# Reordering the first expert selection, its gathers and the first U weights around the query projection

## The chip, the cores and the metric

The kernel runs on one core of one Trainium2 chip. The metric is the device time of one execution in microseconds (us). The engines are PE (matmul; PEld is its weight load), DVE, ACT, POOL and SP, which issues most of the DMAs.

## The reference, cut to what matters

One decoder layer: a token mixer, then a layer of single-neuron experts, then a final norm. Only the expert layer is touched.

```python
qh = (xb @ w_query).reshape(128, 8, 2, 128)          # 8 heads, two halves of a query
s = einsum('thpd,hpnd->thpn', qh, sub_keys)          # scores against 2 x 128 keys of a head
sv, si = top_k(s, 16)                                # the best 16 keys of each half
cand = sv[..., 0, :, None] + sv[..., 1, None, :]     # 16 x 16 sums
cidx = si[..., 0, :, None] * 128 + si[..., 1, None, :]
top_s, pos = top_k(cand, 16); eidx = take(cidx, pos) # 16 experts of each head
gate = softmax(top_s)
act = gelu(einsum('thkd,td->thk', expert_u[eidx], xb))
y = einsum('thk,thkd->td', gate * act, expert_v[eidx])
```

## The kernel before

576 tokens reach the expert layer. For 192 of them (block 0 with 128 tokens, block 1 with 64) the rows of U and V are gathered by index with indirect DMAs that POOL issues. For the other 384 all 16384 experts are computed densely: 128 half steps, each with one chunk of 128 experts of U (function `hidden`), then 128 half steps over V (`experts`), with the gates scattered into a dense array. Every float32 product is made of three matmuls on a high and a low part: ACT copies the weight to the high part, and DVE or POOL subtracts it from the raw weight to get the low part.

`scored` comes just ahead of `hidden`. It goes over two segments of tokens, first 320 (which hold blocks 0, 1 and 2), then 256 (blocks 3 and 4, `o == 0`). In each it goes over 16 chunks `c` of `w_q`: SP loads the raw weight (tag `wr`, 3 buffers), ACT makes `wh` (L133), POOL makes `wl` (L134; DVE does it for the first four chunks of the first segment), PE makes the query (L1092, L1093, then L1095 which needs `wl`), ACT copies it to `qT` (L1097), PE makes the scores of the chunk before (`psc`, L1068), ACT copies them to `sc` (L1071), and DVE finds the best 16 (`top16`, L1020 to L1028, two passes of eight). The instructions here are ordered by the compiler's scheduler, by the order in which they stand in the program and by when it reckons them ready; `after` adds an order by hand.

`select(0)` stands between the two segments: DVE builds candidate sums (L1128 to L1132), takes the best 16 of them (`tv`, `ti`), turns positions into ranks (L1147 to L1158), and looks up the key indices by comparing ranks with 0..15 (`eq`, L1168), multiplying with the indices that ACT has spread out (`sbx`, L1167, in the buffer of `cand`; L1171) and adding in halves (L1177). The softmax (Exp on ACT at L1142, then L1181 to L1183 and L1190) and the indices `gi` (L1189) end it, and four `gather_begin` follow. After the 16th chunk of the second segment, `fetch`, `hi` and `lo` load the first three chunks of U and split them (`lo` of the third is left to `hidden`, where half step h makes the low part of half step h + 2, L1440).

`in_order` fixes the order of PE, DVE, ACT and SP from `hidden` on to that of the program. In each half step `fill` lets DVE do pieces of gathered rows (L1346, L1353) and of the selection of the other blocks, by a written-out cost, ahead of `lo`. At the end, three blocks of 128 output rows are normed: Square on ACT (L1598), a scale, the product on DVE in two halves (L1603), and the output DMAs (L1605), one by SP and one by ACT.

Of the kernel before, what the change touches and what calls it, by code (L numbers as in the profile page):

```python
# [9 lines left out]
F32 = mybir.dt.float32  # L10
F32R = mybir.dt.float32r
BF = mybir.dt.bfloat16
# [10 lines left out]
P = 128  # L23
# [98 lines left out]
class Net:  # L122
# [907 lines left out]
    def scored(self):  # L1030
# [23 lines left out]
        with self.pool("keys", 1, side="right") as kp, self.pool("qw", 2, side="right") as wp:  # L1054
            keys = kp.tile([P, 2 * PH, NK], F32, name="keys")
            nc.sync.dma_start(keys, I["keys"])
            for o, w in SEG:
                here = [b for b, (t0, n) in enumerate(self.blks) if o <= t0 < o + w and b != 1]

                first = 2 * P if o + w == NT else w  # L1060

                def scores(c, q):
                    h, x = divmod(c, 2)
                    pc = self.ps.tile([P, 3, NK], F32, name="psc", tag="ps")
                    sc = wp.tile([P, 2, NK], F32, name="sc", tag="sc", bufs=12)
                    for y, b in enumerate(here):
                        t = (self.blks[b][0] - o) if b else first
                        self.after(mm(pc[:, y, :], q[:, t:t + P], keys[:, c, :], start=True, stop=True), self.last_mm)  # L1068
                    if o + w == NT:
                        self.after(mm(pc[:, 2, :], q[:, P:2 * P], keys[:, c, :], start=True, stop=True), self.last_mm)  # L1070
                    nc.scalar.activation(sc, pc[:, :2], AF.Copy)  # L1071
                    for y, b in enumerate(here):
                        self.top16(P, wp, (sc[:, y, :], sv[:, b, h, x, :], si[:, b, h, x, :]))
                    if o + w == NT:
                        g, k = divmod(h, HB)
                        if g == 0:
                            held[k, x] = wp.tile([P, NK], F32, name="sch", tag="sch", bufs=2 * HB)
                        t, sl = held[k, x], slice(g * NX, (g + 1) * NX)
                        nc.scalar.activation(t[sl], pc[sl, 2], AF.Copy)
                        if g == XG - 1:  # L1080
                            self.top16(P, wp, (t, sv[:, 1, k, x, :], si[:, 1, k, x, :]))

                held = {}
                prev = None
                for c in range(2 * PH):
                    wh, wl = self.weights(I["w_q"][c], lo=nc.vector if o and c < 4 else nc.gpsimd)
                    q = wp.tile([P, 3 * P], F32, name="qT", tag="qT")
                    pq = self.pz.tile([P, 512], F32, name="pq", tag="acc")
                    xs = [(self.xg[0][k], self.xg[1][k]) if o + w == NT else (self.x2h[k][:, o:o + w], self.x2l[k][:, o:o + w])
                          for k in range(KC)]  # L1090
                    for k, (xh, xl) in enumerate(xs):
                        mm(pq[:, :w], wh[:, k, :], xh, start=k == 0, stop=False)  # L1092
                        mm(pq[:, :w], wh[:, k, :], xl, start=False, stop=False)  # L1093
                    for k, (xh, xl) in enumerate(xs):
                        self.last_mm = mm(pq[:, :w], wl[:, k, :], xh, start=False, stop=k == KC - 1)  # L1095
                    n = P + NX if o + w == NT else w
                    nc.scalar.activation(q[:, :n], pq[:, :n], AF.Copy)  # L1097
                    if o + w == NT:
                        nc.scalar.activation(q[:, n:], pq[:, P:w], AF.Copy)
                    if prev:  # L1100
                        scores(*prev)
                    prev = (c, q)
                if o == 0:
                    for s in range(3):
                        self.fetch(s)
                        self.hi(s)
                        if s < 2:
                            self.lo(s)
                scores(*prev)
                if o + w == NT:  # L1110
                    for _ in self.select(0):
                        pass
                    for _ in range(4):
                        self.gather_begin()
                    for d, v in ((self.x2h, self.xg[0]), (self.x2l, self.xg[1])):
                        for k in range(KC):
                            nc.sync.dma_start(d[k][:, o:].bitcast(F32), v[k][:, :MD - o].bitcast(F32))

    def select(self, b):

        nc, wp, sv, si = self.nc, self.sp, self.sv, self.si
        n, H = P, HB if b == 1 else PH
        f = H / PH
        s0, s1 = sv[:n, b, :H, 0, :], sv[:n, b, :H, 1, :]
        cd = wp.tile([P, H, NCAND], F32, name="cand", tag="cand")
        nc.vector.tensor_tensor(cd[:n, :, :TOPK], s0[:, :, 0:1].to_broadcast([n, H, TOPK]), s1, op=ALU.add)  # L1128
# [10 lines left out]

        g = wp.tile([P, H, TOPK], F32, name="gate", tag="gate", bufs=2)  # L1140
        nc.vector.tensor_tensor(g[:n], tv[:n], tv[:n, :, 0:1].to_broadcast([n, H, TOPK]), op=ALU.subtract)
        nc.scalar.activation(g[:n], g[:n], AF.Exp)  # L1142

        def small(name, dt=BF):
            return wp.tile([P, H, TOPK], dt, name=name, tag=name)
# [12 lines left out]
        nc.vector.tensor_add(a[:n], a[:n], t[:n])  # L1158
        yield 1.3 + f
        out = []  # L1160
        sbs = wp.tile([P, H, 2, TOPK], BF, name="sb", tag="sb")
        nc.vector.tensor_copy(sbs[:n], si[:n, b, :H])
        for x, rank in enumerate((a, r)):
            sb = sbs[:, :, x, :]
            e = wp.tile([P, H, TOPK, TOPK], BF, name="eq", tag="eq")
            sx = wp.tile([P, H, TOPK, TOPK], BF, name="sbx", tag="cand")
            nc.scalar.activation(sx[:n], sb[:n, :, :, None].to_broadcast([n, H, TOPK, TOPK]), AF.Copy)  # L1167
            nc.vector.tensor_tensor(e[:n], rank[:n, :, None, :].to_broadcast([n, H, TOPK, TOPK]),  # L1168
                                    self.io16[:n, None].to_broadcast([n, H, TOPK, TOPK]), op=ALU.is_equal)
            yield 0.2 + 1.1 * f  # L1170
            nc.vector.tensor_tensor(e[:n], e[:n], sx[:n], op=ALU.mult)  # L1171
            yield 0.1 + 1.05 * f
            w = TOPK
            v = small(f"ix{x}")
            while w > 1:
                w //= 2
                nc.vector.tensor_add(e[:n, :, :w, :] if w > 1 else v[:n, :, None, :], e[:n, :, :w, :], e[:n, :, w:2 * w, :])  # L1177
                yield (w * H * TOPK) * 0.53e-3 + 0.15
            out.append(v.rearrange("p h k -> p (h k)"))
        sm = wp.tile([P, H], F32, name="gsum", tag="gsum")  # L1180
        nc.vector.tensor_reduce(sm[:n], g[:n], axis=AX.X, op=ALU.add)  # L1181
        nc.vector.reciprocal(sm[:n], sm[:n])
# [1 line left out]
                                       op0=ALU.mult, op1=ALU.mult)  # L1184
        g = g.rearrange("p h k -> p (h k)")
        if b < 2:
            gi = self.gi[b]
            for x in range(2):
                nc.vector.scalar_tensor_tensor(gi[:, x, :], out[x], float(NK), out[1 - x], op0=ALU.mult, op1=ALU.add)  # L1189
            nc.vector.tensor_copy(gi[:, 2, :].bitcast(F32), g)  # L1190
        self.sel[b] = (*out, g)
        yield 1.0

# [118 lines left out]
    def gather_begin(self):  # L1312


        nc = self.nc
        s = self.gstep
        if s == NROW:
            return
        assert s < 4 * GL or 1 in self.sel
        self.gstep += 1  # L1320
        runs = [(0, k) for k in range(4)] + [(1, k) for k in range(XK // GL)] + [(0, k) for k in range(4, PH * TOPK // GL)]
        if s < GL:
            kind, k, r = "u", 0, s
        elif s < 2 * len(runs) * GL - GL:
            k, r = divmod((s - GL) // 2, GL)
            kind, k = ("v", k) if s % 2 else ("u", k + 1)
        else:
            kind, k, r = "v", len(runs) - 1, s % GL
        z, k = runs[k]
        c = k * GL + r  # L1330
        t = self.gp.tile([P, D], F32, name="gr", tag="gr")
        x = 0 if kind == "u" else 1
        src = self.I["v"].rearrange("j i k d -> (j i) (k d)") if x else self.I["ur"]
        nc.gpsimd.indirect_dma_start(out=t, out_offset=None, in_=src,  # L1334
                                     in_offset=bass.IndirectOffsetOnAxis(ap=self.gi[z][:, x, c:c + 1], axis=0))
        self.rows.append((t, kind, z, k, r, c))

    def gather(self):

# [95 lines left out]
            self.ws[s] = [w, None]  # L1435

    def lo(self, s):
        if s < 2 * NK:
            w = self.ws[s][1] = self.up.tile([P, KC, P], F32R, name="ul", tag="ul", bufs=3)
            self.nc.vector.tensor_sub(w, self.raws.pop(s), self.ws[s][0].bitcast(F32))  # L1440

# [88 lines left out]
    def experts(self):  # L1530
# [5 lines left out]
        with ExitStack() as es:  # L1536
# [53 lines left out]
            for b in range(nb):  # L1590
# [10 lines left out]
                for c in range(2):  # L1601
                    sl = slice(c * 512, (c + 1) * 512)
                    nc.vector.scalar_tensor_tensor(o[:, sl], py[b][:, c, :], v, self.gf[:, sl], op0=ALU.mult, op1=ALU.mult)  # L1603
                    if b:
                        (nc.scalar if c else nc.sync).dma_start(self.O["yg"][b * P - ND:(b + 1) * P - ND, sl], o[:, sl])  # L1605
                    else:

                        for n0, n1 in ((16, P), (ND, 16)):
# [98 lines left out]
```

## Time and profile before

| | |
|---|---|
| median of 3 runs | 1939.73 us (1939.11 to 1944.89) |
| the profiled execution | 1941.62 us, its span 1939.4 us |
| PE busy | 1889.3 us (97%) |
| DVE busy | 1592.7 us (82%) |
| ACT busy | 909.2 us (47%) |
| POOL busy | 745.1 us (38%) |
| the chain that ended last | PE 78%, DMA 11%, DVE 9% |

All moments below are us from the start of the span. The second segment of `scored` runs from about 722 to 794 and `hidden` from there to about 1377. A busy share is an average over stages; an engine can be idle for most of the span and still be the one that the others wait for in one stage.

### The profile page before, as it was taken

The page shows a single profiled execution, that of the slowest core. Times are in us where ns is not written, and L with a number is a line of the kernel's source. Part 1 is how long each engine was busy: PE and PEld are TensorE (multiplying, and loading weights), DVE is VectorE, ACT ScalarE, POOL GpSimd, SP SyncE. Part 2 cuts the span into 40 slices and gives each one's busy share as a digit, 9 for nine tenths or more (in the row PEclk, how much of TensorE's full clock was granted, in tenths as well). Part 3 has the DMA queues.
Part 4 walks back from the last instruction along what each step waited for, and adds up shares of the span by engine and source line. Part 5 has one row for each costly group of instructions (what it writes and reads, how often), then busy time and mean ns, then how long its engine had stood idle before and what let it go on. Part 6 is the DMA issues. An engine that isn't in the chain of part 4 may idle for free.

```text
span 1939.4 us, 31893 instructions
## 1 busy us (share of the span) xinstructions
PE 1889.3 (97%) x11759; PEld 1722.4 (89%) x11759; DVE 1592.7 (82%) x2962; ACT 909.2 (47%) x1598; POOL 745.1 (38%) x535
## 2 busy tenths in 40 slices
PE   8999999999999997999999999999999999999997
PEld 7998999788999897999999999999888888877786
DVE  6686776676365779999999999798999888988887
ACT  5542334262324554544878899633333333333333
POOL 1110010300001256345444444366676565665650
PEclk9999999999999998999999999999999999999999
DMA  7355343465554644799999999999999999999992
GB/s 267 103 158 156 87 112 100 140 190 181 175 166 149 211 130 158 248 343 332 348 354 344 398 396 380 376 401 397 402 400 401 397 399 402 400 398 401 399 401 103
DMA packets 219780, 548.08 MB, mean 283 GB/s; under 512 B 31474, under 2 KB 95730, under 8 KB 217960
## 3 DMA queue, kind: packets, MB, share of 16 engines
q1 hardware_dynamic: 163896, 344.17, 50.2%
q0 software_dynamic: 55296, 201.35, 27.0%
q8 instruction: 92, 1.51, 0.3%
q10 hardware_dynamic: 432, 0.54, 0.1%
q14 instruction: 64, 0.52, 0.1%
HBM read 474.89 MB, written 69.77 MB: 281 GB/s over the span
## 4 chain that ended last, share of the span: by engine, by line
PE 78%; DMA 11%; DVE 9%; issue 1%; ACT 1%; SPq 0%; DVEq 0%; ACTq 0%
PE py L1546 18%; PE pz L138 9%; PE pz L140 9%; PE pz L139 9%; PE acc L138 4%; PE acc L140 4%; PE acc L139 4%; DMA wr<-in_v 4%; DMA wj<-wd 3%; PE pw L1264 2%; PE py L664 1%; PE pz L659 1%; PE pq L1095 1%; PE pq L1092 1%; PE pbr L138 1%
## 5 line engine op out<-in xcount | busy, mean ns | idle before, releaser
L1334 POOL DMA_INDIRECT gr<-in_ur,gi x192 | 302.8, 1577 | 265.1 <-DVE yt L1353 200.7
L1334 POOL DMA_INDIRECT gr<-in_v,gi x192 | 300.6, 1566 | 238.8 <-DVE gr L1346 177.3
L1434 ACT ACTIVATE uh<-wr 128x1024 fp32r<-128x1024 f32 x256 | 270.2, 1056 | 217.8 <-PE py L1546 109.7
L138 PE MATMUL pz<-x2h,uh 128*128 128x384 f32 x1024 | 347.0, 339 | 0.0
L140 PE MATMUL pz<-x2h,ul 128*128 128x384 f32 x1024 | 342.9, 335 | 0.0
L139 PE MATMUL pz<-x2l,uh 128*128 128x384 f32 x1024 | 342.9, 335 | 0.0
L1440 DVE TENSOR_TENSOR ul<-wr,uh 128x1024 fp32r<-128x1024 f32 x256 | 313.5, 1225 | 8.9 <-PE pz L140 3.9
L1353 DVE SCALAR_TENSOR_TENSOR yt<-gr,ga,yt 128x1024 f32<-128x1024 f32 x192 | 246.1, 1282 | 7.1 <-DMA gr<-in_v,gi 6.0
L1346 DVE SCALAR_TENSOR_TENSOR gr<-gr,xt 128x1024 f32<-128x1024 f32 x192 | 234.7, 1224 | 12.2 <-DMA gr<-in_ur,gi 12.0
L138 PE MATMUL acc<-xnh,wh 128*128 128x296 f32 (+1 forms) x768 | 232.3, 303 | 8.0 <-ACT xnh L297 6.2
L140 PE MATMUL acc<-xnh,wl 128*128 128x296 f32 (+1 forms) x768 | 233.3, 305 | 0.1
L139 PE MATMUL acc<-xnl,wh 128*128 128x296 f32 (+1 forms) x768 | 232.5, 303 | 0.5 <-DVE xnl L298 0.5
L133 ACT ACTIVATE wh<-wr 128x1024 fp32r<-128x1024 f32 x104 | 110.1, 1059 | 220.7 <-PE acc L139 68.8
L1546 PE MATMUL py<-ul,ah 128*128 128x512 f32 x768 | 201.3, 396 | 4.8 <-DVE ul L1440 4.8
L1546 PE MATMUL py<-uh,ah 128*128 128x512 f32 x768 | 201.6, 396 | 2.6 <-ACT ah L1520 2.0
L1546 PE MATMUL py<-uh,al 128*128 128x512 f32 x768 | 200.5, 395 | 0.0
L140 PEld LDWEIGHTS pz<-x2h,ul 128*128 128x128 f32 x1024 | 192.6, 188 | 0.3 <-DVE ul L1440 0.3
L139 PEld LDWEIGHTS pz<-x2l,uh 128*128 128x128 f32 x1024 | 192.9, 188 | 0.0
L138 PEld LDWEIGHTS pz<-x2h,uh 128*128 128x128 f32 x1024 | 192.6, 188 | 0.1
L1546 PEld LDWEIGHTS py<-ul,ah 128*128 128x128 f32 x768 | 143.5, 188 | 42.1 <-DVE ul L1440 7.8
L1546 PEld LDWEIGHTS py<-uh,ah 128*128 128x128 f32 x768 | 143.2, 188 | 38.2 <-ACT ah L1520 3.5
L1546 PEld LDWEIGHTS py<-uh,al 128*128 128x128 f32 x768 | 144.1, 188 | 35.1
(426 smaller groups left out, 3422.0 us busy)
## 6 DMA issues: line engine op xcount, KB each, us to landing
wr<-in_u SPq DMA_DIRECT2D x128, 512.0 KB
wr<-in_v SPq DMA_DIRECT2D x128, 512.0 KB
gz<-gz SPq DMA_DIRECT2D x96, 384.0 KB
wr<-in_w_in SPq DMA_DIRECT2D x48, 512.0 KB
wd<-wst SPq DMA_DIRECT2D x12, 2048.0 KB
wj<-wd SPq DMA_DIRECT2D x96, 256.0 KB
wr<-in_w_q SPq DMA_DIRECT2D x32, 512.0 KB
wr<-in_w_out SPq DMA_DIRECT2D x16, 512.0 KB
```

What stands on the lines that cost most here:

```text
L133: self.last_hi = self.nc.scalar.activation(hi, src, AF.Copy)
L138: mm(out, wh, xh, start=start, stop=False)
L139: mm(out, wh, xl, start=False, stop=False)
L140: self.last_mm = mm(out, wl, xh, start=False, stop=stop)
L659: mm(pz[:n, h, :n], U[:n, h, :n], X[:n, h, :n], start=True, stop=True)
L1264: nc.tensor.matmul(pw[:, u, :], oh[0][:, t], oh[2 + x][:, t], start=x == 0, stop=x == 1)
L1334: nc.gpsimd.indirect_dma_start(out=t, out_offset=None, in_=src, in_offset=bass.IndirectOffsetOnAxis(ap=self.gi[z][:, x, c:c + 1], axis=0))
L1346: nc.vector.scalar_tensor_tensor(t, t, 1.0, xt, op0=ALU.mult, op1=ALU.mult, accum_out=ga[:, c:c + 1])
L1353: nc.vector.scalar_tensor_tensor(yt, t, ga[:, c:c + 1], yt, op0=ALU.mult, op1=ALU.add)
L1434: self.nc.scalar.activation(w, self.raws[s], AF.Copy)
L1440: self.nc.vector.tensor_sub(w, self.raws.pop(s), self.ws[s][0].bitcast(F32))
L1546: nc.tensor.matmul(py[b][:, c, :], a[:, b * P:(b + 1) * P], w[:, 4 * c:4 * c + 4, :], start=start, stop=stop)
```

## The change

In the first selection the two spreads of the indices move ahead of the search for candidates, into buffers of the gathers' pool (`gr`); `gi` is made ahead of the softmax; and the Exp and the rest of the softmax are put off until after chunk 8 of the second segment (`select` is stopped at `yield 0`). The four gathers come after the 16th chunk and are ordered behind the last `wl` of POOL. The first three chunks of U are loaded and split ahead of chunks 10, 12 and 14 instead of after the 16th, the low part of the third included; `lo` in `hidden` skips what is there. The second output half of the last two blocks is sent by SP instead of ACT. In the selections of the other blocks only the cast of the indices and `gi` stand earlier.

```diff
                 for c in range(2 * PH):
+                    if o == 0 and c in (10, 12, 14):
+                        s = (c - 10) // 2
+                        self.fetch(s)
+                        self.hi(s)
+                        self.lo(s)
...
+                    if o == 0 and c == 8:
+                        for _ in picked:
+                            pass
                 if o == 0:
-                    for s in range(3):
-                        self.fetch(s)
-                        self.hi(s)
-                        if s < 2:
-                            self.lo(s)
+
+                    for _ in range(4):
+                        self.after(self.gather_begin(), self.last_lo)
                 scores(*prev)
                 if o + w == NT:
-                    for _ in self.select(0):
+                    picked = self.select(0, self.gp)
+                    while next(picked):
                         pass
-                    for _ in range(4):
-                        self.gather_begin()
...
-    def select(self, b):
+    def select(self, b, spare=None):
...
+        sbs = wp.tile([P, H, 2, TOPK], BF, name="sb", tag="sb")
+        nc.vector.tensor_copy(sbs[:n], si[:n, b, :H])
+        sxs = []
+        for x in range(2 if spare else 0):
+            sxs.append(spare.tile([P, H, TOPK, TOPK], BF, name="sbx", tag="gr"))
+            nc.scalar.activation(sxs[x], sbs[:, :, x, :, None].to_broadcast([n, H, TOPK, TOPK]), AF.Copy)
...
-        nc.scalar.activation(g[:n], g[:n], AF.Exp)
+        if not spare:
+            nc.scalar.activation(g[:n], g[:n], AF.Exp)
...
-        sbs = wp.tile([P, H, 2, TOPK], BF, name="sb", tag="sb")
-        nc.vector.tensor_copy(sbs[:n], si[:n, b, :H])
...
-            sx = wp.tile([P, H, TOPK, TOPK], BF, name="sbx", tag="cand")
-            nc.scalar.activation(sx[:n], sb[:n, :, :, None].to_broadcast([n, H, TOPK, TOPK]), AF.Copy)
+            if spare:
+                sx = sxs[x]
+            else:
+                sx = wp.tile([P, H, TOPK, TOPK], BF, name="sbx", tag="cand")
+                nc.scalar.activation(sx[:n], sb[:n, :, :, None].to_broadcast([n, H, TOPK, TOPK]), AF.Copy)
...
+        if b < 2:
+            for x in range(2):
+                nc.vector.scalar_tensor_tensor(self.gi[b][:, x, :], out[x], float(NK), out[1 - x], op0=ALU.mult, op1=ALU.add)
+        if spare:
+            yield 0
+            nc.scalar.activation(g[:n], g[:n], AF.Exp)
...
     def lo(self, s):
-        if s < 2 * NK:
+        if s < 2 * NK and not self.ws[s][1]:
...
-                        (nc.scalar if c else nc.sync).dma_start(self.O["yg"][b * P - ND:(b + 1) * P - ND, sl], o[:, sl])
+                        nc.sync.dma_start(self.O["yg"][b * P - ND:(b + 1) * P - ND, sl], o[:, sl])
```

## Rows read from the trace of the kernel before

**Rows 1.** Windows: stretch, length, busy PE, PEld, DVE, ACT, POOL, granted clock, DMA
```profile
722.00:804.00 82.00, 68.37 (x501) 67.71 (x501) 82.00 (x426) 38.05 (x61) 42.49 (x21) 0.90 0.51 174
738.00:745.00 7.00, 0.88 (x7) 0.68 (x6) 7.00 (x52) 4.07 (x6) 0.00 (x0) 0.80 0.22 76
804.00:838.00 34.00, 33.99 (x196) 33.67 (x195) 32.89 (x94) 16.97 (x23) 12.50 (x10) 1.00 0.85 306
```

**Rows 2.** Waits of PE from 722 to 800: total, times, longest
```profile
PE psc L1068 <- ACT qT L1097: 8.3, 2, 6.1
PE pq L1095 <- POOL wl L134: 5.3, 1, 5.3
```

**Rows 3.** Timeline, ACT and POOL: start, length, what, idle before it
```profile
740.90 1.91 ACT L1167 ACTIVATE sbx<-sb 128x2048 bf16<-128x2048 bf16 x1 [5.99 <-DVE mr L1024]
...
728.35 2.59 POOL L134 TENSOR_TENSOR wl<-wr,wh 128x1024 fp32r<-128x1024 f32 x1 [0.48 <-ACT wh L133]
...
760.43 1.15 POOL L1334 DMA_INDIRECT gr<-in_ur,gi  x1 [2.69 <-DVE gi L1189]
```

**Rows 4.** Timeline, half step 10 of hidden: PE behind DVE's low part
```profile
837.57 0.19 PEld L140 LDWEIGHTS pz<-x2h,ul 128*128 128x128 f32 x1 [0.33 <-DVE ul L1440]
```

**Rows 5.** Timeline, DVE in the first selection
```profile
728.79 2.63 DVE L1129 TENSOR_TENSOR cand<-sv 128x448 f32<-128x448 f32 x1
...
731.74 2.49 DVE L1162 CAST sb<-si 128x256 bf16<-128x256 uint32 x1
...
746.79 2.75 DVE L1177 TENSOR_TENSOR eq<-eq 128x1024 bf16<-128x1024 bf16 x1
...
752.33 3.16 DVE L1171 TENSOR_TENSOR eq<-eq,sbx 128x2048 bf16<-128x2048 bf16 x1
...
759.87 0.48 DVE L1189 SCALAR_TENSOR_TENSOR gi<-ix,ix 128x128 int32<-128x128 bf16 x2
```

**Rows 6.** Groups by form, DVE from 800 to 1240: the same instructions later
```profile
L1129 DVE TENSOR_TENSOR cand<-sv 128x448 f32<-128x448 f32 x3 | 1.9, 617 | 0.0
...
L1162 DVE CAST sb<-si 128x256 bf16<-128x256 uint32 x3 | 0.8, 283 | 0.0
...
L1177 DVE TENSOR_TENSOR eq<-eq 128x1024 bf16<-128x1024 bf16 x6 | 4.1, 689 | 0.1
...
L1171 DVE TENSOR_TENSOR eq<-eq,sbx 128x2048 bf16<-128x2048 bf16 x6 | 7.3, 1221 | 0.9 <-ACT sbx L1167 0.8
```

**Rows 7.** Windows of line L134 alone: busy DVE and POOL, with counts
```profile
728.00:760.00 32.00, 0.00 (x0) 16.33 (x6) 0.89 0.34 109
```

**Rows 8.** Timeline, DVE: two instructions beside the last POOL splits
```profile
782.46 2.03 DVE L1346 SCALAR_TENSOR_TENSOR gr<-gr,xt 128x1024 f32<-128x1024 f32 x1
...
786.77 2.48 DVE L1440 TENSOR_TENSOR ul<-wr,uh 128x1024 fp32r<-128x1024 f32 x1
```

**Rows 9.** Timeline: cadence of a chunk on PE, and of its top16 on DVE
```profile
786.27 1.12 PE L1095 MATMUL pq<-x2h,wl 128*128 128x256 f32 x8
...
789.59 1.12 PE L1095 MATMUL pq<-x2h,wl 128*128 128x256 f32 x8
...
761.44 0.27 DVE L1020 MAX8 sv<-sc 128x8 f32<-128x128 f32 x1
...
763.78 0.28 DVE L1020 MAX8 sv<-sc 128x8 f32<-128x128 f32 x1
```

**Rows 10.** Timeline: first load of U on SP, and ACT's split of it
```profile
780.12 12.96 SPq L1423 DMA_DIRECT2D wr<-in_u  x9
...
783.31 1.06 ACT L1434 ACTIVATE uh<-wr 128x1024 fp32r<-128x1024 f32 x1 [1.69 <-DMA wr<-in_u]
```

**Rows 11.** Timeline, the tail
```profile
1929.08 0.63 PE L1546 MATMUL py<-uh,al 128*128 128x512 f32 x2
...
1931.04 0.35 ACTq L1605 DMA_DIRECT2D out_yg<-yo  x1
1931.43 1.02 ACT L1598 ACTIVATE yo<-py 128x1024 f32<-128x1024 f32 x1 [2.95 <-DVE yo L1603]
```

More of the change, by code (lines that the diff above doesn't have):

```diff
@@ L1186, in select @@
         if b < 2:
[L1187 to L1190, printed above, removed]
+            nc.vector.tensor_copy(self.gi[b][:, 2, :].bitcast(F32), g)
         self.sel[b] = (*out, g)
@@ L1333, in gather_begin @@
         src = self.I["v"].rearrange("j i k d -> (j i) (k d)") if x else self.I["ur"]
-        nc.gpsimd.indirect_dma_start(out=t, out_offset=None, in_=src,
-                                     in_offset=bass.IndirectOffsetOnAxis(ap=self.gi[z][:, x, c:c + 1], axis=0))
+        ins = nc.gpsimd.indirect_dma_start(out=t, out_offset=None, in_=src,
+                                           in_offset=bass.IndirectOffsetOnAxis(ap=self.gi[z][:, x, c:c + 1], axis=0))
         self.rows.append((t, kind, z, k, r, c))
+        return ins
     def gather(self):
```

## The prediction, made blind

> **What bounds the kernel now.** I read the waits of PE first, because PE is busy for 97% of the span and a change can only win where it stands still. Around the second segment of `scored` there are three such places [rows 2]: twice the scores wait for `qT` (6.1 us, and 2.2 us of the 8.3 in total), and once the query waits 5.3 us for `wl`. Together 13.6 us, and all three are touched. The first is ACT standing in front of `sbx` for 5.99 us, until the candidates' buffer is free, with `qT` queued behind it; the second is POOL, which has four gathers, begun as soon as `gi` is there, ahead of the next `wl` [rows 3]. In the seven microseconds of the first wait PE is busy for 0.88, and the granted clock of that window is 0.80 on average, where 1.00 is the level of 2.4 GHz and 0.5 that of 1.2 [rows 1].
>
> The windows then show the other side: from 722 to 804, while PE is busy for 68.37 of 82 us, DVE is busy for all 82, and from 804 to 838, where PE is full, DVE still has 32.89 of 34 [rows 1]. Whether PE's idle time is worth anything depends on which of the two the next stage waits for. In `hidden`, half step h needs the low part `ul` of its chunk, DVE makes these in a fixed order between other work, and in half step 10 PE's weight load begins after 0.33 us of waiting for just that subtraction [rows 4]. So at 837 us PE has no lead over DVE left to give: a PE that comes 13 us earlier waits for DVE there, and a DVE that comes later moves PE one for one. The stretch from 728 to 838 is a DVE stretch, and I sum DVE's time in it.
>
> **DVE in the first selection.** Its work stays the same: the same cast, comparisons, products and adds, the four softmax operations (about 1 us) put behind chunk 8 but not removed, and three low parts before `hidden` instead of two before and one in it. What can change is the time that DVE's instructions stand still inside. Five in the first selection are far longer than the same forms later: the candidates 2.63 us for 0.617, the cast 2.49 for 0.283, an add 2.75 for 0.689 (the second add of this form likewise), a product 3.16 for 1.221 [rows 5, 6]. Each began while POOL was inside a `wl` subtraction. The losses are 2.01, 2.21, 2.06, 1.94 and about 2.0, together 10.2 us, 2.05 for each collision. The searches for the best 16 (MAX8 and its kin) keep their length beside POOL. Two later ones are a gathered row (2.03 us for 1.22, loss 0.8) and the first `ul` (2.48 for 1.22, loss 1.3), both beside the last `wl` [rows 8]: 2.1 us. DVE thus loses 12.3 us to POOL before, and that is all that this change could win on DVE.
>
> The Trainium skill (SBUF — State Buffer, section Who interferes with whom) says that a DVE instruction with two inputs in SBUF and a GpSimd instruction that reads SBUF exclude each other for a whole instruction, that a cast can take part too in a fast mode, and that other instructions with one input do not. The trace agrees for the five forms above; by this rule the short rank operations with two inputs (L1152 to L1158), which met no `wl` before, would collide as well, and the count below would be 9 to 10 instead of 8, some 3 us more.
>
> How many collisions will there be? Before, six `wl` fell into the 32 us of the first selection [rows 7], and five of them collided; there were so few because PE, and with it the order of splits, stood still for 6.1 us in that stretch. A chunk at full pace takes 789.59 − 786.27 = 3.32 us [rows 9], so without the wait there is a `wl` every 3.32 us. The selection without collisions and softmax is 31.9 (from 728.4, just ahead of the candidates, to the end of `gi` at 760.3 [rows 5]) − 10.2 − 1.0 = 20.7 us. Its eight searches are at most half a chunk's pair of searches each (a chunk takes 763.78 − 761.44 = 2.34 us [rows 9]), so under 9.4 us in all, and two `wl` fall in there for nothing. With n collisions it lasts 20.7 + 2.05n, and n = (20.7 + 2.05n) / 3.32 − 2 gives n = 11. Two things keep it lower: ACT's two spreads of 1.91 us stand together ahead of chunk 1's `qT` and delay the first `wl` (ACT is busy for some 1.8 of 3.32 us of a chunk, so it takes two or three chunks to catch up), and from chunk 12 on the query's loads are short of buffers (below). Bounds: 3, if DVE's chain of dependent instructions keeps POOL out, and 11. I take 8, nearer to the regular cadence: 16.4 us for 10.2, **+6.2 us**. Of the three `ul` that now stand between chunks, I let one collide (1.3 us) where 2.1 us were lost before, bounds 0 and 3.8: **−0.8 us**. Moving the spreads ahead wins DVE nothing else, since it did not wait for them.
>
> **ACT and POOL.** The 5.99 us wait at `sbx` goes: a spread now needs only the cast, which stands first in the selection. Exp and its table load leave the path of `qT` and come back at chunk 8, where `tv` has long been there. The gathers behind the last `wl` end the 5.3 us wait. Behind them on POOL stands nothing but further gathers; DVE's first gathered row is wanted in half step 0. All this gives PE up to 13.6 us, which I count as 0, since DVE carries the stretch; the bound on the other side is the rival below.
>
> **Loads of U between chunks.** Each takes one of the three `wr` buffers until DVE has made its low part. DVE reaches the first only after the searches of chunks up to 8, some 18 us behind the end of `gi`, while PE is already at chunk 12. Two buffers are then held, the third goes round by itself, and the third load of U takes it too: the last two `w_q` wait for DVE. A load takes 783.31 − 780.12 = 3.2 us to ACT's split of it [rows 10]; then 1.06 on ACT, some 2.4 on POOL (16.33 for six [rows 7], waits included) and 1.1 on PE [rows 9]. So PE arrives at half step 0 close to when it did before, and not 13 us earlier. As long as it arrives no more than a few us later, with the low parts of half steps 0 to 2 made, DVE stays the one that sets half step 3; I count 0 here, with a price in the rivals.
>
> **The tail.** Square of the third output block waits on ACT behind the DMA issue of the second (1931.04), which waits for DVE's product; PE had ended at 1929.71 [rows 11]. With SP as issuer ACT begins some 1.7 us earlier, DVE's product of the second block, for which that issue waited, is then just past, and SP's two extra issues cost it 0.35 us each with nothing urgent behind: **−1.6 us** (bounds −1.7 and 0). Casts and `gi` that stand earlier in the other selections move nothing.
>
> **Sum.** +6.2 − 0.8 − 1.6 = +3.8 us. The profiled execution took 1941.62 us with a span of 1939.4; the sum belongs to the span, and the same 3.8 on the median of 1939.73 gives 1943.5 us.
>
> **Rivals.**
> *PE sets it after all* (faster). If the scheduler puts DVE's low parts for half steps 3 on ahead of the searches of the last chunks, whose results are wanted much later, DVE's backlog does not hold PE: −13.6 − 1.6 = −15.2, 1924.5 us. For it: three low parts are ready early. Against it: DVE has no idle time at all in rows 1, and the three buffers hold PE back anyway. It decides from where the low part of half step 3 ends ahead of PE's end of half step 2. Chance 0.08.
> *Fewer collisions* (faster). The early cast and spreads shift `wl` into the searches, and dependent DVE chains keep POOL waiting: 3 collisions and none at the low parts give −4.1 − 2.1 − 1.6 = −7.8, 1931.9 us. Against it: two `wl` fit into the searches, and before they did for one. Chance 0.18.
> *The buffers hold PE* (slower). From `gi` at 765.5 (760.3 + 6.2 − 1.0) DVE needs 18 us of searches and 1 of softmax to the first `ul`, which ends at 785.7; chunk 14's load, splits and product end at 793.4, chunk 15's at 800 behind the next buffer. Half step 0 then begins some 6 us behind 794, and the gathers, behind the last `wl`, reach DVE's fixed order late by 2 to 3 us more. That is +8 to +9 before the tail, 1947 us; with 11 collisions it is 1951. It decides once PE's half step 3 begins later than DVE's low part for it. Chance 0.30.
> *DVE carries it* as summed, between 0 and +5.8: chance 0.44.
>
> **Numbers.** About 0.3% (5.8 us) is what a measurement of this kernel tells from no change. The forecast of 1943.5 is +0.2%: same 0.43. Slower by more takes the buffers' case and a bit of the sum's upper half: 0.33. Faster takes the two faster rivals but the smallest wins: 0.24. The range 1931 to 1952 leaves out the first rival and the worst of the third; the likeliest case by itself spans 1938 to 1946.
>
> **What would show it.** Right: PE's waits at `qT` and `wl` gone, new ones at chunks 12 to 15 with SP's `w_q` loads waiting for DVE's `ul`; DVE without idle time to 804 and beyond; `gi` ended later than 760.3 and seven or more DVE instructions of 2 us too long beside `wl`; Square of the third block right behind PE's last product. Wrong: `gi` earlier than 760, half step 3 of `hidden` earlier than 808 (seven half steps ahead of 837; 196 products, 24 to a half step, in the 34 us of rows 1 make 4.16 us each), or DVE with gaps between 728 and 804.

## The result, and the profile after

The change makes the kernel slower: 1949.63 us, median of 6 runs (1946.27 to 1952.98), against 1938.94 for the kernel before, median of 6 (1936.86 to 1944.89). The ratio is 1.0054 (95% interval 1.0036 to 1.0071). The profiled execution took 1949.87 us with a span of 1947.6 (before 1941.62 and 1939.4). The forecast was 1943.5 with a range of 1931 to 1952: the right side and inside the range, but the mechanism that adds most was priced at nothing.

Windows of the kernel after, with the stretches and columns of [rows 1]:

```profile
722.00:804.00 82.00, 62.85 (x477) 61.30 (x477) 75.39 (x369) 35.77 (x59) 40.42 (x20) 0.90 0.39 130
738.00:745.00 7.00, 7.00 (x61) 7.00 (x61) 7.00 (x26) 4.45 (x9) 4.68 (x3) 1.00 0.47 156
804.00:838.00 34.00, 27.94 (x148) 27.62 (x147) 32.26 (x113) 13.73 (x18) 10.68 (x9) 0.90 0.86 310
```

The hole that the change aims at is closed: from 738 to 745 PE is busy throughout, at a granted clock of 1.00, where it had 0.88 of 7 us. Yet PE does less in the whole stretch (62.85 us for 68.37), and DVE, which had no idle time, now stands still for 6.61 of 82 us. The waits tell where (PE and DVE, 650 to 830: total, times, longest):

```profile
PE pq L1097 <- ACT wh L133: 17.6, 3, 13.2
PE pz L140 <- DVE ul L1458: 6.1, 1, 6.1
...
PE psc L1068 <- ACT qT L1102: 0.5, 1, 0.5
...
DVE gr L1364 <- DMA gr<-in_ur,gi: 7.7, 1, 7.7
```

The wait for `qT` fell from 8.3 us to 0.5 [rows 2]. In its place PE waits 17.6 us for a `wh`, DVE 7.7 us for a gathered row, and then PE 6.1 us for DVE's low part. The first of these is not what counts, as the runs below show; the other two are one chain. The timeline shows it on POOL, DVE and PE (start, length, idle time before it):

```profile
786.57 1.06 ACT L1452 ACTIVATE uh<-wr 128x1024 fp32r<-128x1024 f32 x1 [14.25 <-DMA wr<-in_u]
...
789.19 2.37 POOL L134 TENSOR_TENSOR wl<-wr,wh 128x1024 fp32r<-128x1024 f32 x1 [14.94 <-ACT wh L133]
793.26 3.40 POOL L134 TENSOR_TENSOR wl<-wr,wh 128x1024 fp32r<-128x1024 f32 x1 [1.70 <-ACT wh L133]
796.83 1.14 POOL L1351 DMA_INDIRECT gr<-in_ur,gi  x1 [0.17 <-DVE mr L1024]
...
805.19 1.23 DVE L1364 SCALAR_TENSOR_TENSOR gr<-gr,xt 128x1024 f32<-128x1024 f32 x1 [7.70 <-DMA gr<-in_ur,gi]
...
816.65 1.20 DVE L1458 TENSOR_TENSOR ul<-wr,uh 128x1024 fp32r<-128x1024 f32 x1
...
817.91 0.69 PE L140 MATMUL pz<-x2h,ul 128*128 128x384 f32 x1 [6.06 <-DVE ul L1458]
```

`gi` is there at 764.4, but the gathers go out at 796.83, behind the last split (before: 760.43 [rows 3]). The row lands 8.34 us later, and DVE, whose order is fixed, stands in front of it for 7.70 us with searches and low parts queued behind. The low part of half step 3 ends at 817.85, and PE takes it up 0.06 us later. PE has then stood still for 6.06 us, and it comes back at a granted clock of 0.50, the level of 1.2 GHz (window, columns as above):

```profile
817.91:821.00 3.09, 3.09 (x10) 3.09 (x11) 2.92 (x14) 1.80 (x3) 0.94 (x1) 0.50 0.80 265
```

A product of 0.34 us takes 0.52 there. From its first product with that low part to its next half step PE needs 6.24 us, against 3.82 in e1 (below), where it did not wait: 2.4 us more.

DVE in the first selection after (all instructions that are far longer than their form is elsewhere, and the last of the stretch):

```profile
728.34 2.29 DVE L1140 TENSOR_TENSOR cand<-sv 128x128 f32<-128x128 f32 x1
...
741.16 2.23 DVE L1169 TENSOR_TENSOR rb<-rb,rw 128x128 bf16<-128x128 bf16 x1
743.31 2.43 DVE L1171 TENSOR_TENSOR ra<-ra,rt 128x128 bf16<-128x128 bf16 x1
745.94 3.16 DVE L1182 TENSOR_TENSOR eq<-ra,io 128x2048 bf16<-128x2048 bf16 x1
...
751.48 2.35 DVE L1191 TENSOR_TENSOR eq<-eq 128x512 bf16<-128x512 bf16 x1
753.96 2.27 DVE L1191 TENSOR_TENSOR eq<-eq 128x256 bf16<-128x256 bf16 x1
...
758.15 3.39 DVE L1185 TENSOR_TENSOR eq<-eq,sbx 128x2048 bf16<-128x2048 bf16 x1
...
763.92 0.47 DVE L1196 SCALAR_TENSOR_TENSOR gi<-ix,ix 128x128 int32<-128x128 bf16 x2
```

Seven collisions (instructions stretched beside a split) instead of five, each again about 2.05 us over its form's own length [rows 5, 6].

The tail (PE, ACT, SP) became shorter as forecast, by more:

```profile
1939.71 0.63 PE L1564 MATMUL py<-uh,al 128*128 128x512 f32 x2
...
1940.38 1.02 ACT L1616 ACTIVATE yo<-py 128x1024 f32<-128x1024 f32 x1 [1.26 <-PE py L1564]
...
1941.01 3.74 SPq L1623 DMA_DIRECT2D out_yg<-yo  x4
1944.85 0.40 SPq L1636 DMA_DIRECT2D out_y<-y  x1
```

Square of the third block follows PE's last product directly (before it began 1.72 us behind it [rows 11]). From the end of that product (1940.34) to the end of the span it is 7.3 us; before it was 1939.4 − 1929.71 = 9.7.

### The profile page after: what moved, and what is told of

Read it like the earlier page. It is cut to its first block, busy times and chain, and to the rows that moved or that the text cites. A ratio compares the mean times of both kernels' runs of the same rounds, so it can differ in the third digit from the quotient of the medians.

```text
span 1947.6 us, 31888 instructions
## 1 busy us (share of the span) xinstructions
PE 1889.6 (97%) x11759; PEld 1721.8 (88%) x11759; DVE 1596.3 (82%) x2962; ACT 908.3 (47%) x1598; POOL 741.8 (38%) x535
## 4 chain that ended last, share of the span: by engine, by line
PE 77%; DMA 11%; DVE 9%; issue 1%; ACT 1%; POOL 0%; SPq 0%; DVEq 0%; ACTq 0%
PE py L1564 17%; PE pz L138 9%; PE pz L140 9%; PE pz L139 9%; PE acc L138 5%; PE acc L140 5%; PE acc L139 5%; DMA wr<-in_v 4%; DMA wj<-wd 4%; PE pw L1281 2%; PE py L664 1%; PE pz L659 1%; PE pq L1100 1%; PE pq L1097 1%; PE pbr L138 1%
## 5 line engine op out<-in xcount | busy, mean ns | idle before, releaser
L1458 DVE TENSOR_TENSOR ul<-wr,uh 128x1024 fp32r<-128x1024 f32 x256 | 312.2, 1219 | 10.5 <-PE pz L140 3.9
```

## A common zero for the traces

The spans of single executions scatter by several us, and the scatter lies ahead of the change. DVE's first candidate sum of the selection starts at 728.39 us before, 728.34 after, and between 725.69 and 734.26 in the ten experiments, although DVE's instructions up to it stand in the same order, but for two: the selection's new order puts the cast, and with it one search step, 0.41 us together, ahead of it (727.93 to 728.34 in the kernel after). Anchored times of kernels with the new order are therefore some 0.4 us too small beside those of before, e4 and e7, which have the old one. I count from that instruction in every trace, and call these times anchored. "Low part 3" is the end of DVE's `ul` for half step 3; "product" is the end of PE's last large product; "long" is the number of stretched instructions in the selection; "tail" runs from product to the end of the span. "Ratio" is to the kernel before, run beside it on the same chip, with its 95% interval.

| kernel | long | `gi` ends | first gathered row | low part 3 | product | tail | end | ratio |
|---|---|---|---|---|---|---|---|---|
| before | 5 | 31.96 | 54.07 | 79.43 | 1201.32 | 9.69 | 1211.01 | |
| after | 7 | 36.05 | 76.85 | 89.51 | 1212.00 | 7.26 | 1219.26 | 1.0054 |
| e1_gathers_early | 4 | 29.90 | 58.88 | 79.33 | 1201.44 | 7.33 | 1208.77 | 0.9999 (0.9984 to 1.0013) |
| e2_u_old_place | 11 | 44.04 | 75.51 | 89.47 | 1210.05 | 7.29 | 1217.34 | 1.0043 (1.0028 to 1.0058) |
| e3_select_only | 4 | 29.90 | 52.25 | 76.94 | 1198.56 | 9.52 | 1208.08 | 0.9993 (0.9981 to 1.0006) |
| e4_tail_only | 5 | 31.97 | 54.08 | 79.42 | 1202.41 | 7.31 | 1209.72 | 0.9993 (0.9979 to 1.0006) |
| e5_select_tail | 4 | 29.91 | 52.35 | 77.04 | 1200.43 | 7.26 | 1207.69 | 0.9972 (0.9956 to 0.9987) |
| e6_late_gathers_fence | 4 | 29.92 | 73.20 | 85.85 | 1208.99 | 7.63 | 1216.62 | 1.0029 (1.0014 to 1.0044) |
| e7_no_splits | 0 | 21.73 | 43.82 | 67.24 | 1189.49 | 9.58 | 1199.07 | 0.9946 (0.9923 to 0.9970) |
| e8_u_low_pool | 4 | 29.92 | 52.24 | 80.65 | 1201.98 | 7.79 | 1209.77 | 0.9981 (0.9966 to 0.9995) |
| e9_u_low_pool_cast_late | 4 | 29.90 | 52.25 | 75.92 | 1199.79 | 7.74 | 1207.53 | 0.9991 (0.9977 to 1.0006) |
| e10_fence_ahead | 1 | 23.70 | 33.45 | 74.90 | 1197.82 | 7.29 | 1205.11 | 0.9974 (0.9962 to 0.9987) |

For every kernel the anchored difference of the ends lies in the interval of its timed runs. Two traces with the same work up to low part 3 agree there to 0.1 us (before and e4, e3 and e5); their last products differ by 1.1 and 1.9 us, so the end column is good to some 2 us and the low part column, between kernels of the same order, to a tenth.

## The experiments

At first I held that the wait for the gathered row was the main loss, that the loads of U caused it by holding back the last split, and that the collisions added 4 us. The first four runs put each edit back or did it alone.

**e1: the gathers back behind `gi`**

```
-                if o == 0:
-                    for _ in range(4):
-                        self.after(self.gather_begin(), self.last_lo)
...
                     while next(picked):
                         pass
+                    for _ in range(4):
+                        self.gather_begin()
```

> The changed kernel with the four first gathers back at their old place, right behind the selection's index sum and ordered behind no weight split. Theory A (VectorE sets the end, and its 7.70 us of waiting for the first gathered row is the largest term): the wait is gone, the low part of weight 3 ends some 6 us sooner than in the changed kernel (bounded below by TensorE, whose half step 0 still starts at about 798), and the span is 1941.5 to 1942.5 us, some 2 to 3 above the kernel before and 5 to 6 below the changed one. Rival B (the collisions of VectorE with GpSimd's splits are the loss, and the wait for the gathers only shows slack): the span stays within 2 us of the changed kernel's 1947.6. Rival C (TensorE's 13.2 us of waiting for a chunk whose weight buffer holds a U weight moves the end by itself): stays at 1946 or more too, since that wait is left in.

All 10 us at low part 3 went with this one edit (89.51 to 79.33), more than the 6 that I expected. Rival C falls: PE still waits 11.5 us for `wl` and 4.3 for `wh` in this kernel, and its end is 10.5 us ahead of the changed one's. Rival B this run cannot decide, because of something unforeseen: the collisions fell as well, from seven to four (e6 parts the two). ACT and POOL show why (timeline):

```profile
747.59 1.04 ACT L133 ACTIVATE wh<-wr 128x1024 fp32r<-128x1024 f32 x1
...
738.57 7.13 POOL L134 TENSOR_TENSOR wl<-wr,wh 128x1024 fp32r<-128x1024 f32 x3 [2.31 <-ACT wh L133]
756.02 1.15 POOL L1349 DMA_INDIRECT gr<-in_ur,gi  x1 [10.32 <-DVE gi L1194]
```

The first gather stands at the head of POOL's queue for 10.32 us, waiting for `gi`, and the splits behind it do not run, although the `wh` of the next is there at 748.63. In the changed kernel there is nothing to stop them, and the splits at 751 and 758 fall on the adds and the second product. The Trainium skill (PSUM — Partial Sum Buffer, section Engine vs sequencer instructions) states that GpSimd's queue is a strict first-in first-out one; the trace agrees, with 10.32 us of an idle POOL. In the kernel before, the longest pause of the splits in the selection, 8.89 us, had another cause: `wh`, which stood on ACT behind the wait for the candidates' buffer [rows 3]:

```profile
746.27 2.72 POOL L134 TENSOR_TENSOR wl<-wr,wh 128x1024 fp32r<-128x1024 f32 x1 [8.89 <-ACT wh L133]
```

**e2: the first U weights back behind the chunks, the gathers still behind the last split**

```
-                    if o == 0 and c in (10, 12, 14):
-                        s = (c - 10) // 2
-                        self.fetch(s)
-                        self.hi(s)
-                        self.lo(s)
...
                 if o == 0:
+                    for s in range(3):
+                        self.fetch(s)
+                        self.hi(s)
+                        if s < 2:
+                            self.lo(s)
```

> The changed kernel with the fetch and the parts of the first three U weights back behind the 16 query chunks (two low parts there, as before); the gathers still stand behind the last weight split. Theory A: no chunk waits for a buffer, the last split ends near 789 instead of 796.66, the gathered row lands near 797 and VectorE waits 0 to 1.5 us for it; the collisions stay, so the span is 1941.5 to 1944. Rival B (collisions alone): within 2 us of 1947.6. Rival C: below 1940, since only the buffers' wait is gone and the rest was free.

My theory missed: low part 3 ends at 89.47, no sooner than in the changed kernel. No split waits for a buffer any more, the last one ends at 43.89 instead of 68.32, the gathers go out at 44.07, and DVE does not wait for a row at all. But now a split runs every 3.3 us through the second half of the selection too (POOL, then DVE of this kernel):

```profile
754.73 2.56 POOL L134 TENSOR_TENSOR wl<-wr,wh 128x1024 fp32r<-128x1024 f32 x1 [0.79 <-PE psc L1068]
757.82 2.81 POOL L134 TENSOR_TENSOR wl<-wr,wh 128x1024 fp32r<-128x1024 f32 x1 [0.53 <-ACT wh L133]
761.13 2.41 POOL L134 TENSOR_TENSOR wl<-wr,wh 128x1024 fp32r<-128x1024 f32 x1 [0.51 <-ACT wh L133]
...
755.14 3.22 DVE L1185 TENSOR_TENSOR eq<-eq,sbx 128x2048 bf16<-128x2048 bf16 x1
758.56 2.62 DVE L1191 TENSOR_TENSOR eq<-eq 128x1024 bf16<-128x1024 bf16 x1
761.36 2.46 DVE L1191 TENSOR_TENSOR eq<-eq 128x512 bf16<-128x512 bf16 x1
```

Eleven collisions: 44.04 − 31.96 = 12.08 us for six more than before, 2.01 each. The prediction's formula for an undisturbed cadence of splits gave just n = 11. The U loads, which were to be the culprit, had kept splits away by holding the buffers of the `w_q` loads. So the theory became (A'): the gathers' old place holds POOL's queue until `gi` is done; moving them costs either the collisions that follow, or the wait for the row, in proportions that the loads decide.

**e3: the selection's order alone**

Kernel before, with `select` and its two calls as changed; gathers, first U weights and outputs as before:

```
-                    for _ in self.select(0):
+                    picked = self.select(0, self.gp)
+                    while next(picked):
                         pass
...
+                    if o == 0 and c == 8:
+                        for _ in picked:
+                            pass
```

> The kernel before with only the selection's new order (both index spreads ahead, in two gather buffers; the softmax behind chunk 8); gathers, first U weights and outputs at their old places. It prices the collisions. Theory A: 7 or 8 instructions of the selection stand in a split's time where 5 did, VectorE is some 4 us later at the end of the index sum, and the span is 1942 to 1944 (before 1939.4). Rival B: 1946 or more. Against both: if TensorE's 8.3 us of waiting for VectorE's scores was what counted, the span falls below 1938.

Wrong sign again: four collisions, not seven or eight. `gi` ends 2.06 us earlier, low part 3 2.49 us earlier, some 0.4 us less if the cast ahead of the zero is counted. At low part 3 the selection's new order is a gain by itself; the interval of the timed runs also allows no change.

**e4: the outputs alone**

```
-                        (nc.scalar if c else nc.sync).dma_start(...)
+                        nc.sync.dma_start(...)
```

> The kernel before with only the outputs of the last two blocks issued by SyncE alone. From the changed kernel's tail, where the time from TensorE's last large product to the end of the span is 7.3 us against 9.7: the span is 1.6 to 2.4 us shorter, 1937.0 to 1937.8. If the gain of the tail is a matter of where the other kernel's last block stood, nothing is gained.

The tail is 7.31 us for 9.69, and 7.3 to 7.8 in all eight experiments with SP as issuer, against 9.5 to 9.7 in the two others with the old tail: 1.7 to 2.4 us gained. The interval of the timed runs does not tell so little from nothing.

The second set tested A'.

**e5: selection and tail without the other two edits**

Edits of e3 and e4 together.

> The kernel before with the selection's new order and with SyncE's outputs; gathers and first U weights at their old places. With the gathers-early run, the U-weights-back run and the changed kernel it makes a square of two places by two places. Theory A' (the gathers at their old place hold GpSimd's queue until the index sum is done, so that no split runs beside the second half of the selection): 4 stretched instructions, the index sum ends 29.9 us after the first candidate sum (before 31.96, changed kernel 36.05), the low part of weight 3 ends 76.9 us after it (before 79.43), the end of the span 1206.8 us after it (before 1211.0): about 4 us faster, 1936. Rival (the selection's order gains only as much as its own run showed by chance): not faster than 0.1%.

1935.89 us against 1940.07, an interval of 0.9956 to 0.9987: faster than the kernel before, and 1936 was expected. It closes the square of two edits at low part 3: 77.04 with neither, 79.33 with the U loads moved, 89.47 with the gathers moved, 89.51 with both. The move of the gathers costs 12.4 or 10.2 us, that of the U loads 2.3 or nothing. Of the 2.3, DVE shows 0.95 as a wait for the score of a late chunk; the rest I have not taken apart.

**e6: late gathers, but POOL's queue held**

```
                     while next(picked):
                         pass
+                    stop = self.sp.tile([P, 1], I32, name="stop", tag="stop")
+                    nc.gpsimd.tensor_copy(stop, self.gi[0][:, 1, :1])
```

> The changed kernel with one more GpSimd instruction, a copy of one column of the index sum, at the gathers' old place; the gathers stay behind the last split. The copy holds GpSimd's queue as the gathers did, so it parts the two things that the gathers' move did. Theory A' (both count, and the later one sets the end): 4 stretched instructions instead of 7 and the index sum 29.9 us after the first candidate sum instead of 36.05, but the gathers still go out some 66 us after it or later, the first gathered row lands 8.4 us behind that, VectorE waits 10 us or more for it, and the low part of weight 3 ends 86 to 89 us after the first candidate sum (changed kernel 89.51, gathers early 79.33): at most 3 us gained. Rival B (the stretched instructions are the loss): 83.4 and 6 us gained. Rival D (the late gathers are harmless once the queue is held): 79 to 80 and 9 to 10 us gained.

```profile
761.26 0.19 POOL L1121 COPY stop<-gi 128x1 int32<-128x1 int32 x1 [10.30 <-DVE gi L1198]
...
795.83 1.15 POOL L1353 DMA_INDIRECT gr<-in_ur,gi  x1 [0.17 <-issue]
...
804.48 1.22 DVE L1366 SCALAR_TENSOR_TENSOR gr<-gr,xt 128x1024 f32<-128x1024 f32 x1 [7.45 <-DMA gr<-in_ur,gi]
```

The copy does hold the queue, and the collisions are four again, 6.1 us won at `gi`. Only 3.66 reach low part 3, since DVE still stands 7.45 us before the row. The theory's range (86 to 89) is missed by 0.15 us, and its wait of 10 us or more did not come, since the last split ended earlier as well (64.38 for 68.32). B and D are farther off: the late row remains as a bound of its own. Between e1 (79.33), e6 (85.85) and the changed kernel (89.51) the gathers' price of 10.2 us parts into 6.5 for the late row and 3.7 for the three collisions on top of it.

**e7: no split beside the selection**

```
-                    wh, wl = self.weights(I["w_q"][c], lo=nc.vector if o and c < 4 else nc.gpsimd)
...
+                        nc.scalar.activation(wh, raw, AF.Copy)
+                        nc.scalar.activation(wl, raw, AF.Copy, scale=2.0 ** -13)
```

> The kernel before with the low parts of the second segment's 16 query weights made by ScalarE as a scaled copy of the weight; it leaves out their subtraction, so that GpSimd does no elementwise work beside the first selection. Price of the splits to VectorE. Theory: no instruction of the selection is stretched (5 were), the index sum ends 21 to 22 us after the first candidate sum instead of 31.96, and what VectorE wins by it reaches the low part of weight 3 only as far as TensorE's chunks let it: 70 to 74 us after the first candidate sum instead of 79.43, and the span 5 to 9 us shorter than before. Rival: the long instructions are long by their own access and stay: no change of the index sum, span within 1.5 us of before.

```profile
727.83 0.62 DVE L1137 TENSOR_TENSOR cand<-sv 128x448 f32<-128x448 f32 x1
728.75 0.30 DVE L1170 CAST sb<-si 128x256 bf16<-128x256 uint32 x1
...
741.62 0.69 DVE L1185 TENSOR_TENSOR eq<-eq 128x1024 bf16<-128x1024 bf16 x1
...
745.10 1.22 DVE L1179 TENSOR_TENSOR eq<-eq,sbx 128x2048 bf16<-128x2048 bf16 x1
```

The long instructions of [rows 5] are 0.62, 0.30, 0.69 and 1.22 us here, the length of [rows 6]. `gi` ends 10.23 us earlier and low part 3 12.19 earlier: the forecast's 10.2 and 12.3 to a tenth. The end is 11.9 us earlier, more than the 5 to 9 that I expected; TensorE's chunks did not hold it back.

**e8 and e9: the first three low parts of U by POOL**

```
-            self.nc.vector.tensor_sub(w, ...)
+            (self.nc.gpsimd if s < 3 else self.nc.vector).tensor_sub(w, ...)
...
-                        if s < 2:
-                            self.lo(s)
+                        self.lo(s)
```

> The select-and-tail kernel with the low parts of the first three U weights made by GpSimd behind its last split instead of by VectorE (1.22 us each on VectorE where nothing stretches them, 2.4 us each on GpSimd). Theory A' (VectorE sets the end in this stretch): the low part of weight 3 ends 3.7 us sooner, 73 us after the first candidate sum, and the span is 2 to 3.7 us shorter than that of the select-and-tail kernel, 1932 to 1934. Rival: TensorE has become the bound there (its half steps 0 to 2 go 12.5 us without a stop) and less than 1 us is won.

A miss: low part 3 ends 3.6 us later than in e5 (80.65 for 77.04), not 3.7 sooner. DVE, POOL and PE:

```profile
786.75 8.48 DVE L1131 CAST sb<-si 128x128 bf16<-128x128 uint32 x1
...
785.75 2.41 POOL L134 TENSOR_TENSOR wl<-wr,wh 128x1024 fp32r<-128x1024 f32 x1
788.10 7.05 POOL L1456 TENSOR_TENSOR ul<-wr,uh 128x1024 fp32r<-128x1024 f32 x3
...
810.46 1.23 DVE L1456 TENSOR_TENSOR ul<-wr,uh 128x1024 fp32r<-128x1024 f32 x1
...
811.74 0.69 PE L140 MATMUL pz<-x2h,ul 128*128 128x384 f32 x1 [5.49 <-DVE ul L1456]
```

A cast of this form takes 0.22 us in e6; here it lasts 8.48, until the last of four subtractions in a row is over. The first `ul` that DVE makes here, at 810.46, is the one of half step 3, and PE waits 5.49 us for it. The 84.86 in the expectation of e9 is the end of DVE's next one, for half step 4. e9 put this cast of the later selections back at its old place:

> The kernel with GpSimd's low parts of the first three U weights, in which one 128x128 cast of the second selection stood 8.48 us beside four of GpSimd's subtractions in a row; here the cast of the later selections is back at its old place, behind the ranks, and only the first selection's is ahead. If the cast was the loss and nothing takes its place: the low part of weight 3 ends 8 us sooner, 76.5 us after the first candidate sum against 84.86, and the end is 1203 to 1206 after it (select-and-tail kernel 1207.7). If what comes next on VectorE falls beside the same subtractions (the three candidate sums of the second selection, two-input instructions too): two or three of them take over 2 us, the low part of weight 3 ends at 80 to 83, and the end is not below 1207.

```profile
784.71 2.03 DVE L1139 TENSOR_TENSOR cand<-sv 128x64 f32<-128x64 f32 x1
...
789.50 2.13 DVE L1143 TENSOR_TENSOR cand<-sv 128x32 f32<-128x32 f32 x1
```

The second branch held: two candidate sums took over 2 us, the low part of half step 4, by which the expectation counts, ends at 80.12, and the end is 1207.53. Low part 3 itself ends at 75.92, 1.1 us ahead of e5's where 3.7 had been hoped for: much of the work that leaves DVE for POOL comes back as collisions.

**e10: the gathers three splits further ahead**

e5 with chunk 6's split, and so the splits behind it, ordered behind the fourth gather:

```
+                    if o == 0 and c == 6:
+                        self.after(self.last_lo, self.fence)
...
+                    for _ in range(4):
+                        self.fence = self.gather_begin()
```

> The select-and-tail kernel with the gathers ordered three splits further ahead on GpSimd (chunk 6's split and all behind it wait for the index sum). Theory A': one instruction of the selection is stretched instead of four, and the index sum ends 23.8 us after the first candidate sum instead of 29.91. What follows of it: three splits more lie behind the index sum, so the last split ends 60 to 62 after it instead of 57.2, and TensorE's chunks at 3.3 us each feed VectorE's searches late; the low part of weight 3 ends 73 to 77 (now 77.04), the end at 1204 to 1208. Rival: the chunks eat the gain and more, the low part of weight 3 ends after 78 and the end is over 1208.5.

```profile
749.48 1.15 POOL L1352 DMA_INDIRECT gr<-in_ur,gi  x1 [13.57 <-DVE gi L1197]
...
PE pq L1097 <- POOL wl L134: 13.5, 1, 13.5
```

One collision, `gi` at 23.70 (expected 23.8), low part 3 at 74.90, end 1205.11. PE stands still for 13.5 us in one piece, longer than in any wait that the change removed, and this has the earliest end of the kernels that compute everything: 1934.45 us for 1940.43. Its end is 2.6 us ahead of e5's in the traces, little more than their scatter; the timed intervals of the two do not part. PE takes up low part 3 at 76.58, 1.68 us behind its end: here PE is the later one.

## Why the prediction was right, and where it was not

Counted at low part 3, the change costs 10.08 us: 36.05 − 31.96 = 4.09 from two more collisions, 7.70 from the wait for the row, less 2.1 us for the low parts and the row that no longer collide, with 0.4 left over. PE's half step 4 begins 12.1 us later than before, 2.4 of it from the lower clock behind its wait. At PE's last product it is 10.68; how much was made up in between is within the scatter. The tail gives back 2.43, and the end is 8.25 us later; the forecast was 3.8. That the time lies inside the range is in part luck: 7.7 us were left out, and the three terms that were counted came out 4.2 us lower together than forecast.

- **DVE carries the stretch from 728 to 838, PE's idle time is worth nothing.** Right for the change: PE waits for DVE's low part of half step 3. Counted from before, the last product moves as low part 3 does, within 2.0 us, in every kernel. But "nothing" is too strong. After waits for `wl` of 10.9 us (e1, e9) and 13.5 us (e10) PE takes up low part 3 1.6 to 1.7 us behind its end and waits for no low part up to half step 13, so that there PE's lateness bounds, by that much.
- **DVE loses 12.3 us to POOL before.** Right: 12.19 in e7.
- **Eight collisions after, +6.2 us.** Nearly: seven, +4.09. The Trainium skill (SBUF — State Buffer, section Who interferes with whom) was right on the short rank operations: L1169 and L1171 took 2.23 and 2.43 us for about 0.2. My words on instructions with one input were too short, though: the section counts copies and tensor-scalar operations in a fast mode as well as casts, which no run here tests. The reason I gave for the few collisions before, that "there were so few because PE, and with it the order of splits, stood still for 6.1 us", stands for that kernel, where POOL was idle for 8.89 us. What I concluded from it failed: the 6.1 us wait is gone in e1, e3 and e5, and the collisions fell to four. What limits them in the new order is the gather at the head of POOL's queue, for 10.32 us; in the kernel before it had held the queue for only 2.69 us [rows 3].
- **The failed step** is the one on the gathers: "Behind them on POOL stands nothing but further gathers; DVE's first gathered row is wanted in half step 0", counted as 0. One of the prediction's own signs of being wrong came true with it: DVE has a gap between 728 and 804, the 7.70 us that begin at 797.49. The step looked at what stands behind the gathers in their new place and not at what would have stood behind them in the old one: the splits that they held back in e1, for 10.32 us. And it took the row's due time by the half step, while DVE's order has it ahead of the last searches. Its price is 10.2 us (e1 against the changed kernel), of which the row alone makes 6.5 (e6 against e1). The rival on buffers had the right chain, from the U loads by the last split to a late gather, but put the row 2 to 3 us late where it was 7.7, and took PE's lateness as the loss.
- **Low parts between chunks, −0.8.** 1.22 us each, none collided, nor did the gathered row: −2.1.
- **The tail, −1.6.** −2.4: also the time behind the Square became shorter.
- **U's loads counted at 0.** Right beside late gathers (0.04 us at low part 3), but by luck: without them four more collisions (7.99 us at `gi`) stand in place of the 7.70 us wait for the row. Beside early gathers they cost 2.3.

## What to carry to other kernels

An instruction that waits at the head of an in-order queue is also a fence for all that is queued behind it: before it is moved, ask what it has been holding back and whom that would disturb. Look for a transfer's consumer in its engine's actual order, not in the step for which the data are nominally needed. And where two traces differ ahead of the change, count both from an instruction that the change cannot have moved.

## What the hardware showed that I had not expected

A DVE instruction beside POOL's splits is not always through after one of them. Beside three splits in a row DVE got one instruction done between each two (2.23, 2.43 and 3.16 us in the changed kernel), but the cast in e8 stood through what was left of one subtraction and three more, 8.48 us; in e9 a candidate sum beside the same three got through after one (2.13 us). The Trainium skill (SBUF — State Buffer, section Who interferes with whom) lets the later one of the two engines wait for a whole instruction of the other; here it waited for four. What decides between the two cases I have not tested.
